# Opening of a decoder layer: modulation rows asked for one block sooner, ahead of the weight rows

## The chip, the core and the metric

The kernel runs on one core of a Trainium2 chip. The core has a matmul engine (TensorE, PE in the profile), a vector engine (VectorE, DVE), a scalar engine (ScalarE, ACT), a general engine (GpSimd, POOL) and a synchronization engine (SyncE, SP), which here only issues DMA transfers. The metric is the device time of one execution in microseconds, as the median over runs.

## The reference

One decoder layer over 512 positions with 1024 channels, all float32. What matters here is its beginning: a condition vector gives six modulation vectors, the first two of which shift and scale the normed input, and the result is multiplied by the columns of a large input projection.

```python
cond = jax.nn.silu(c)
mod = cond @ ada_w[l] + ada_b[l]
sh1, sc1, g1, sh2, sc2, g2 = jnp.split(mod[:, None, :], N_MOD, axis=-1)
u = rms_norm(x, mix_pre_g[l]) * (1.0 + sc1) + sh1
proj = u @ w_in[l]
...  # an mLSTM group and a convolution group, an output projection, then a ConvFFN
```

## The kernel before

Everything is computed with the channels on the 128 partitions. A product in float32 is made of three matmuls: each operand is split into a high part (fp32r, ACT) and a low part (the rest, POOL or DVE), and high by high, low by high and high by low are added up.

The stage that the change touches is called the opening. After the input is loaded, normed and turned, the opening goes over KT = 8 blocks of 128 input channels. For block k it needs

- the **modulation rows** of the block: `first_load(k)` loads two pieces of 512 KB (scale and shift, the two halves of one tile of 2048 columns) with two DMAs on SP's queue, line L245. The profile calls them `ada<-in_adaT`. The tiles lie in four buffers, two of the pool `raws` and two of the pool `early_raws`, so the load for block k takes the buffer of block k-4 and waits until the sums over it are done;
- the **weight rows** of the block: `w_rows(k)` loads 384 KB, the rows of the first G0 = 6 column tiles of the gated convolution's projection, with one DMA on SP's queue, line L343. The profile calls them `wglu<-in_w_glu`. There are two buffers (ADAS = 2), so the load for block k waits until the weight rows of block k-2 are split.

What is done with them: `w_part` splits the weight rows into high parts (ACT, L191, 512 columns and 256 columns) and low parts (POOL, L192). `part_sum` multiplies each modulation row by the condition and sums (DVE, L330, twice a block), `part_gains` makes a scale and a shift of the sums (L335, L336). ACT makes the high part of u from the turned input (L405), and again the full value (L406), and the low part is their difference (POOL, L407; in the last block DVE). Then `glu_pass` issues 18 matmuls for the block (L350): three passes over six banks that collect the sum over all blocks. On ACT, DVE and POOL the opening's instructions run in the order of the program (`in_order`), on ACT the two splits of a block ahead of its u. SP and PE run in the order of the program throughout. So SP, when the buffer of a load is not free, holds back all that stands behind it.

After the eight blocks the remaining projections follow (`proj`, line L210), then attention, convolution, output projection and the ConvFFN. The first load after the opening is that of the weights of column tile 3 (`glu_weights`, L199), which takes a buffer of `raws`.

Of the kernel before, what the change touches and what calls it, by code (L numbers as in the profile page):

```python
# [20 lines left out]
KT = D // P  # L21
# [34 lines left out]
def decoder_layer(ctx, tc, w_glu0, x, c, adaT, vecs, w_glu, w_qko, w_v0, w_vo, w_out, w_up, w_down, out):  # L56
# [93 lines left out]
    def vcols(name, i, n):  # L150
        a = VEC[name][0] + i
        return vec[:, a : a + n]
# [88 lines left out]
    def first_load(k):  # L241

        r = (raws if k % 4 < 2 else early_raws).tile([P, 2048], F32, tag="raw", name=f"ada{k}")
        for i in range(2):
            nc.sync.dma_start(r[:, i * D : (i + 1) * D], adaT[k][:, i * D : (i + 1) * D])  # L245
        first.append(r)
# [4 lines left out]
    def turn_x(j, tt):  # L251
        PE.transpose(xT_ps[j][:, tt * P : (tt + 1) * P], xn[tt][j // NT][:, j % NT * P : (j % NT + 1) * P], ident)
# [43 lines left out]
    def x_out(j, eng):  # L296
        if eng is S:
            S.activation(xr[j], xT_ps[j], AF.Copy)
        else:
            V.tensor_copy(xr[j], xT_ps[j])  # L300
# [23 lines left out]
    def part_sum(k, i):  # L324

        if i == 0:
            parts[k] = small.tile([P, 2], F32, tag="adap", name=f"adap{k}"), small.tile([P, 2], F32, tag="gsk", name=f"gsk{k}")
        part = parts[k][0]
        junk = small.tile([P, D], BF16, tag="junk", bufs=1, name=f"junk{k}_{i}")
        V.scalar_tensor_tensor(out=junk, in0=first[k][:, i * D : (i + 1) * D], scalar=1.0, in1=cps, op0=ALU.mult, op1=ALU.mult,  # L330
                               accum_out=part[:, i : i + 1])

    def part_gains(k):
        part, gsk = parts[k]
        V.tensor_scalar(out=gsk[:, :1], in0=part[:, :1], scalar1=bp1[:, k : k + 1], scalar2=g32[:, k : k + 1], op0=ALU.add, op1=ALU.mult)  # L335
        V.tensor_scalar(out=gsk[:, 1:], in0=part[:, 1:], scalar1=vcol("ada_b", 2 * k + 1), scalar2=None, op0=ALU.add)  # L336
# [4 lines left out]
    def w_rows(k):  # L341
        rows0[k] = adas.tile([P, D], F32, tag="ada", name=f"wglu0_{k}")
        nc.sync.dma_start(rows0[k][:, : G0 * P], w_glu0[k])  # L343

    def w_part(k, a, n):
        wk.append(w_split(rows0[k][:, a : a + n], f"wglu0_{k}_{a}"))

    def glu_pass(ps, i, p):
        a, b = ((0, 0), (1, 0), (0, 1))[p]
        PE.matmul(ps, blk(wk, i)[a], u[k][b], start=k == 0 and p == 0, stop=k == KT - 1 and p == 1)  # L350

    for k in range(KT):
        wk = []

        if k == 0:
            w_rows(0)
            first_load(1)
        if k + 1 < KT:
            w_rows(k + 1)
        if k + 2 < KT:  # L360
            first_load(k + 2)
        if k == 2:
            nc.sync.dma_start(vec[:, FIRST:], vecs[:, FIRST:])
        hi, lo = u[k]
        if k == 0:
            w_part(k, 0, T)
            part_sum(k, 0)
            part_sum(k, 1)
            part_gains(k)
            sc, sh = parts[k][1][:, :1], parts[k][1][:, 1:]  # L370
            S.activation(hi, xT_ps[0], AF.Identity, scale=sc, bias=sh)
            x_out(1, V)
            x_out(2, S)
            x_out(3, S)
            V.tensor_scalar(out=xr[0], in0=xT_ps[0], scalar1=sc, scalar2=sh, op0=ALU.mult, op1=ALU.add)
            G.tensor_tensor(out=lo, in0=xr[k], in1=hi.bitcast(F32), op=ALU.subtract)
            w_part(k, T, (G0 - 4) * P)
            x_out(4, V)
            x_out(5, S)
            for i, p in ((0, 0), (1, 0), (0, 1), (1, 1), (2, 0), (2, 1), (3, 0), (3, 1)):  # L380
                glu_pass(banks0[i], i, p)
            for j in range(6, KT):
                for tt in range(NT):
                    turn_x(j, tt)
            wk, first_wk = [], wk
            w_part(1, 0, T)
            wk, next_wk = first_wk, wk
            x_out(6, S)
            x_out(7, S)
            for i in range(4):  # L390
                glu_pass(banks0[i], i, 2)
            for p in range(3):
                for i in range(4, G0):
                    glu_pass(banks0[i], i, p)
        else:
            if k == 1:
                wk = next_wk
            else:
                w_part(k, 0, T)
            w_part(k, T, (G0 - 4) * P)  # L400
            part_sum(k, 0)
            part_sum(k, 1)
            part_gains(k)
            sc, sh = parts[k][1][:, :1], parts[k][1][:, 1:]
            S.activation(hi, xr[k], AF.Identity, scale=sc, bias=sh)  # L405
            S.activation(xr[k], xr[k], AF.Identity, scale=sc, bias=sh)  # L406
            (V if k == KT - 1 else G).tensor_tensor(out=lo, in0=xr[k], in1=hi.bitcast(F32), op=ALU.subtract)  # L407
            if k < KT - 1:
                for p in range(3):
                    for i, ps in enumerate(banks0):  # L410
                        glu_pass(ps, i, p)
            else:
                for i, ps in enumerate(banks0):
                    glu_pass(ps, i, 0)
                for i, ps in enumerate(banks0):
                    glu_pass(ps, i, 2)
                    glu_pass(ps, i, 1)
        if k == 6:
            V.tensor_scalar(out=cvw, in0=vcols("cv_dw_w", 0, CK * KT), scalar1=0.5, scalar2=None, op0=ALU.mult)
            V.tensor_scalar(out=ghalf, in0=vcols("ml_norm_g", 0, KT), scalar1=0.5, scalar2=None, op0=ALU.mult)  # L420
# [958 lines left out]
```

## Time and profile before

| | |
|---|---|
| median of 3 runs | 768.74 us (768.34 to 769.21) |
| profiled execution | 769.16 us |
| its span from first to last instruction | 767.4 us |
| PE busy | 756.0 us, 99% of the span |
| DVE, ACT, POOL busy | 576.6, 410.7, 516.5 us |
| mean granted clock of PE | 0.999 |
| loads of the opening on SP's queue | 16 modulation loads of 512 KB, 8 weight loads of 384 KB |
| first matmul of block 0, of the opening | 15.29 us |
| end of the opening's matmuls (first matmul of L210) | 51.02 us |

Times in the profile are microseconds from the first instruction; busy is the time in which an engine had an instruction running. A row of the timeline or of the chain gives start, length, engine, line and what is written from what. A row of the waits names the engine and line that waited, what it waited for, the total, the number of times and the longest. A row that describes transfers ends with the time from the issue to the landing of the data. The chain of work that ended last is followed back from the last instruction, at each step to what released it.

### The profile page before, as it was taken

How to read it: one execution, taken by the hardware profiler on the slowest of the kernel's cores; microseconds unless marked ns; L12 is line 12 of the kernel's file. 1: busy time of each engine (PE TensorE's matmuls, PEld its weight loads, DVE VectorE, ACT ScalarE, POOL GpSimd, SP SyncE). 2: the span in 40 equal slices, each digit the busy share in tenths (PEclk: the TensorE clock that was granted, in tenths of full speed). 3: DMA queues.
4: the chain of work that ended last, by engine and by line, in shares of the span. 5: the costliest groups of instructions: out<-in, count | busy, mean ns of one | idle time of the engine just before them, and what ended most of it. 6: DMA issues, size and time to landing. Idle time of an engine off the chain costs nothing.

```text
span 767.4 us, 10129 instructions
## 1 busy us (share of the span) xinstructions
PE 756.0 (99%) x3480; PEld 625.1 (81%) x3480; DVE 576.6 (75%) x837; ACT 410.7 (54%) x778; POOL 516.5 (67%) x428
## 2 busy tenths in 40 slices
PE   7999999999999999999999999999999999999996
PEld 5778898878788788888889988888888888888885
DVE  6669999979979696476989978675684775654547
ACT  6675428585665655573345444443534444566633
POOL 4779849796494872645631179786887884599943
PEclk9999999999999999999999999999999999999999
DMA  8973313411131241655965755666767565796273
GB/s 317 349 281 113 112 56 117 158 56 56 55 111 56 98 168 64 235 199 168 365 222 183 271 210 191 240 219 247 262 231 275 187 239 185 271 397 241 93 249 135
DMA packets 40136, 147.32 MB, mean 192 GB/s; under 512 B 3826, under 2 KB 5266, under 8 KB 30484
## 3 DMA queue, kind: packets, MB, share of 16 engines
q1 hardware_dynamic: 27524, 96.59, 34.9%
q10 hardware_dynamic: 12560, 50.08, 18.3%
q8 instruction: 27, 0.44, 0.2%
q14 instruction: 25, 0.20, 0.1%
HBM read 126.59 MB, written 20.07 MB: 191 GB/s over the span
## 4 chain that ended last, share of the span: by engine, by line
PE 93%; DMA 4%; POOL 1%; ACT 1%; issue 0%; DVEq 0%; SPq 0%; DVE 0%; POOLq 0%; ACTq 0%
PE up L210 31%; PE dn L210 13%; PE qko L210 13%; PE vo L210 9%; PE glu L210 7%; PE mixa L210 6%; PE mixb L210 6%; DMA wglu<-in_w_glu 3%; PE o L562 2%; PE s L551 2%; PE v L210 2%; PE glu L350 1%; DMA xn<-in_x 1%; PE xT L992 0%; PE hT L593 0%
## 5 line engine op out<-in xcount | busy, mean ns | idle before, releaser
L774 DVE SCALAR_TENSOR_TENSOR cv<-gt,cvw,cv 128x485 f32<-128x485 f32 (+24 forms) x200 | 137.2, 731 | 2.1 <-ACT cv L762 0.8
L770 POOL TENSOR_TENSOR cs<-cs,cs 128x510 f32<-128x510 f32 (+3 forms) x32 | 42.1, 1316 | 0.2
L192 POOL TENSOR_TENSOR wup_0l<-wup,wup_0h 128x512 fp32r<-128x512 f32 x18 | 25.0, 1389 | 19.4 <-ACT wup_0h L191 19.3
L210 PE MATMUL up<-u2h,wup_0h 128*128 128x512 f32 (+1 forms) x96 | 35.8, 373 | 0.0
L210 PE MATMUL up<-u2h,wup_0l 128*128 128x512 f32 (+1 forms) x96 | 35.7, 371 | 0.0
L210 PE MATMUL up<-u2h,wup_512h 128*128 128x512 f32 (+1 forms) x96 | 35.6, 371 | 0.0
L210 PE MATMUL up<-u2l,wup_512h 128*128 128x512 f32 (+1 forms) x96 | 35.6, 371 | 0.0
L210 PE MATMUL up<-u2h,wup_512l 128*128 128x512 f32 (+1 forms) x96 | 35.6, 371 | 0.0
L210 PE MATMUL up<-u2l,wup_0h 128*128 128x512 f32 (+1 forms) x96 | 35.6, 371 | 0.0
L210 PE MATMUL up<-u2h,wup_1024h 128*128 128x512 f32 (+1 forms) x92 | 35.0, 381 | 0.0
L210 PE MATMUL up<-u2l,wup_1024h 128*128 128x512 f32 (+1 forms) x92 | 34.9, 380 | 0.0
L210 PE MATMUL up<-u2h,wup_1536l 128*128 128x512 f32 (+1 forms) x92 | 34.9, 380 | 0.0
L210 PE MATMUL up<-u2h,wup_1536h 128*128 128x512 f32 (+1 forms) x92 | 34.9, 380 | 0.0
L210 PE MATMUL up<-u2l,wup_1536h 128*128 128x512 f32 (+1 forms) x92 | 34.9, 380 | 0.0
L210 PE MATMUL up<-u2h,wup_1024l 128*128 128x512 f32 (+1 forms) x92 | 34.9, 380 | 0.0
L176 DVE SCALAR_TENSOR_TENSOR junk<-ada,cb 128x1024 bf16<-128x1024 f32 x20 | 29.9, 1493 | 2.6 <-DMA ada<-in_adaT 2.5
L768 ACT ACTIVATE cs<-gt,cvw 128x511 f32<-128x511 f32 (+4 forms) x40 | 27.1, 713 | 6.1 <-POOL cs L770 3.5
L192 POOL TENSOR_TENSOR wup_1536l<-wup,wup_1536h 128x512 fp32r<-128x512 f32 x18 | 24.6, 1365 | 6.0 <-ACT wup_1536h L191 5.4
L191 ACT ACTIVATE wup_512h<-wup 128x512 fp32r<-128x512 f32 x22 | 13.8, 629 | 25.7 <-PE up L210 20.9
L192 POOL TENSOR_TENSOR wup_1024l<-wup,wup_1024h 128x512 fp32r<-128x512 f32 x18 | 23.6, 1314 | 5.0 <-ACT wup_1024h L191 5.0
L330 DVE SCALAR_TENSOR_TENSOR junk<-ada,cps 128x1024 bf16<-128x1024 f32 x16 | 19.5, 1220 | 9.8 <-DMA ada<-in_adaT 9.2
L1113 DVE TENSOR_TENSOR b<-b 128x512 f32<-128x512 f32 x11 | 19.4, 1762 | 8.6 <-POOL b L1112 8.6
(1097 smaller groups left out, 2726.8 us busy)
## 6 DMA issues: line engine op xcount, KB each, us to landing
wup<-in_w_up SPq DMA_DIRECT2D x22, 1024.0 KB, 5.0
b<-in_w_down ACTq DMA_DIRECT2D x11, 1024.0 KB, 5.1
spill_t<-b ACTq DMA_DIRECT2D x11, 1024.0 KB, 3.9
ada<-in_adaT ACTq DMA_DIRECT2D x20, 512.0 KB, 4.8
wqko<-in_w_qko SPq DMA_DIRECT2D x9, 1024.0 KB, 4.8
ada<-in_adaT SPq DMA_DIRECT2D x16, 512.0 KB, 7.5
wo<-in_w_out SPq DMA_DIRECT2D x8, 1024.0 KB, 5.5
wvo<-in_w_vo SPq DMA_DIRECT2D x6, 1024.0 KB, 4.8
```

What stands on the lines that cost most here:

```text
L176: t = V.scalar_tensor_tensor(out=junk, in0=r, scalar=1.0, in1=cb, op0=ALU.mult, op1=ALU.mult, accum_out=mod[:, i : i + 1])
L191: S.activation(hi[:, :n], src, AF.Copy)
L192: (eng or G).tensor_tensor(out=lo[:, :n], in0=src, in1=hi[:, :n].bitcast(F32), op=ALU.subtract)
L210: PE.matmul(ps, l, r, start=start and i == 0, stop=stop and i == 2, skip_group_check=again)
L330: V.scalar_tensor_tensor(out=junk, in0=first[k][:, i * D : (i + 1) * D], scalar=1.0, in1=cps, op0=ALU.mult, op1=ALU.mult, accum_out=part[: ...
L350: PE.matmul(ps, blk(wk, i)[a], u[k][b], start=k == 0 and p == 0, stop=k == KT - 1 and p == 1)
L551: PE.matmul(sp[:, :n], ks[d][:, cc * P : (cc + 1) * P], qs[d][:, cc * P :], start=d == 0, stop=d == 1)
L562: PE.matmul(o[:, : DH + 2], E[h][cc][:, a : a + P], vs[h][cc], start=cc == 0, stop=cc == tt)
L768: S.activation(t[:, d:], cvx[j][:, : T - d], AF.Copy, scale=w(CK - 1 - d))
L770: G.tensor_tensor(out=side[:, d:], in0=side[:, d:], in1=t[:, d:], op=ALU.add)
L774: tap = V.scalar_tensor_tensor(out=cp[:, d:], in0=cvx[j][:, : T - d], scalar=w(CK - 1 - d), in1=cp[:, d:], op0=ALU.mult, op1=ALU.add)
L1113: V.tensor_tensor(out=b22, in0=b22, in1=b11, op=ALU.subtract)
```

## The change

In the loop over the blocks, the loads are issued in another order. Before, block k asked for the weight rows of block k+1 and then for the modulation rows of block k+2. After, block 0 also asks for the modulation rows of block 3, and each later block k asks first for the modulation rows of block k+3 and then for the weight rows of block k+1. What is loaded, into which buffers, and what is computed stays as it is.

```diff
         if k == 0:
             w_rows(0)
             first_load(1)
-        if k + 1 < KT:
+        if k == 0:
+            w_rows(1)
+            first_load(2)
+        if k + 3 < KT:
+            first_load(k + 3)
+        if 0 < k < KT - 1:
             w_rows(k + 1)
-        if k + 2 < KT:
-            first_load(k + 2)
         if k == 2:
             nc.sync.dma_start(vec[:, FIRST:], vecs[:, FIRST:])
```

## The prediction

> **What bounds the kernel now.** I read the page's busy times first, then the chain that ended last, then the waits of the matmul engine after the opening, then the opening alone: chain, transfers, throughput.
>
> ```profile
> span 767.4 us, 10129 instructions
> PE 756.0 (99%) x3480; PEld 625.1 (81%) x3480; DVE 576.6 (75%) x837; ACT 410.7 (54%) x778; POOL 516.5 (67%) x428
> PE 93%; DMA 4%; POOL 1%; ACT 1%; issue 0%; DVEq 0%; SPq 0%; DVE 0%; POOLq 0%; ACTq 0%
> ```
>
> PE is the bound: 93% of the chain is PE, and the rest has to be sought where PE does not yet run without a break. The waits of PE show two in the opening and, asked from 52 us to the end, none:
>
> ```profile
> PE glu L350 <- ACT uh L371: 1.3, 1, 1.3
> PE glu L350 <- ACT uh L405: 0.9, 1, 0.9
> ```
>
> So whatever PE loses or wins before its last L350 matmul passes on to the end, one for one. The chain in time from 17 to 51 us:
>
> ```profile
> 17.41 0.74 POOL wglu_512l L192
> 18.16 0.02 issue
> 18.18 3.60 DMA wglu<-in_w_glu
> 21.77 0.02 issue
> 21.80 0.64 ACT wglu_0h L191
> ...
> 24.52 7.04 DMA wglu<-in_w_glu
> ...
> 41.03 0.63 ACT wglu_0h L191
> ...
> 42.72 8.45 PE glu L350 x36
> ```
>
> The reader sees a loop: weight rows of block k land, ACT and POOL split them, the buffer comes free, SP issues the weight rows of block k+2, and these wait in the queue for their turn. The chain runs through the weight rows (wglu), never through the modulation rows (ada). The last wait ends at 42.72, with block 6; block 7 starts at 46.94 and the stage ends at 51.02.
>
> **The change, part by part.** It adds and removes no instruction and no byte: on SP's queue two modulation loads per block (512 KB each) change places with one weight load. I write m_k for the pair of modulation loads of block k, w_k for its weight load. Before: m2, w2, m3, w3, m4, vec, w4, m5, w5, m6, w6, m7, w7. After: m2, m3, m4, w2, m5, w3, vec, m6, w4, m7, w5, w6, w7.
>
> *What it wins.* SP stands at w2 until POOL has finished with the first buffer (the 17.41 row), and nothing is queued behind it. The second half of m2 and w2:
>
> ```profile
> 11.39 0.33 SPq L245 DMA_DIRECT2D ada<-in_adaT  x1
> ada<-in_adaT SPq DMA_DIRECT2D x1, 512.0 KB, 8.5
> 18.18 0.33 SPq L343 DMA_DIRECT2D wglu<-in_w_glu  x1
> wglu<-in_w_glu SPq DMA_DIRECT2D x1, 384.0 KB, 3.6
> ```
>
> m2 lands at 11.39 + 8.5 = 19.9, and w2, with an empty queue, 3.6 after its issue. Throughput (columns: window, its length, granted clock, DMA share, GB/s):
>
> ```profile
> 11.00:18.40 7.40, 1.00 1.03 411
> 18.50:20.00 1.50, 1.00 0.71 141
> 37.00:41.00 4.00, 1.00 0.86 263
> ```
>
> Between 18.5 and 20 the engines moved 141 GB/s where 411 is usual: 1.5 x (1 - 141/411) = 1.0 us of transfer time lost. With m3 and m4 issued ahead of the wait this hole is filled. Also the vector engine's waits for modulation rows shrink:
>
> ```profile
> ACT wglu_0h L191 <- DMA wglu<-in_w_glu: 12.6, 8, 3.4
> DVE junk L330 <- DMA ada<-in_adaT: 9.2, 7, 2.1
> ```
>
> I cost that at nothing. ACT scales block k into u behind its split of w_k, so the later of the two rows decides, and that is the wglu row. Its cover is w_k arriving late; were w_k early, the modulation sums would be last.
>
> *Can the moved loads go out in time?* m4 needs the buffer of m0, read by block 0's sums, the last of which ends at 14.05:
>
> ```profile
> 13.97 0.08 DVE L330 DVE_READ_ACCUMULATOR junk<-ada,cps 128x1 f32 x1
> 4.86 0.33 SPq L245 DMA_DIRECT2D ada<-in_adaT  x1
> ada<-in_adaT SPq DMA_DIRECT2D x1, 512.0 KB, 6.5
> 7.59 0.33 SPq L245 DMA_DIRECT2D ada<-in_adaT  x1
> ada<-in_adaT SPq DMA_DIRECT2D x1, 512.0 KB, 7.5
> ```
>
> m2's second half went out at 11.39, when the first half of m0, eight transfers ahead of it in issue order, had landed (4.86 + 6.5 = 11.4). By that rule m4's second half waits for the first half of m1: 7.59 + 7.5 = 15.1. SP is back at the wait for w2 long before 18.18, which therefore stays its issue time. Nothing waits behind it that did not before.
>
> *What it costs.* At 18.18 the queue now holds the rest of m2 and all of m3 and m4. Transfers of this queue landed in the order of issue, so w2 follows four more halves. These and w2 are 4 x 0.524 + 0.393 = 2.49 MB, at 411 GB/s 6.1 us after m2's 19.9: w2 lands at 26.0 instead of 21.8. That is the lower end. For the upper end:
>
> ```profile
> 27.32 0.63 ACT L191 ACTIVATE wglu_0h<-wglu 128x512 fp32r<-128x512 f32 x1 [3.03 <-DMA wglu<-in_w_glu]
> 29.02 1.21 PE L350 MATMUL glu<-uh,wglu_0h 128*128 128x512 f32 x4
> q8 instruction: 1, 0.02, 6.2%
> ```
>
> From w2 (21.8, in the chain) to w3 there were 5.5 us for 1.44 MB, which at 411 GB/s take 3.5. The 2.0 too many lie in the very time in which w2 will now be on its way. The last row, of the transfers from 24.3 to 25.3, names one contributor, an instruction fetch that took a turn on one of the sixteen engines, and a load has landed only when all sixteen are done. Some of the 2.0 came of the queue's fresh start at 19 and will go. So w2 lands between 26.0 and 28.0; I take 26.8, a little under the middle of the two, for that share.
>
> The Trainium skill, "DMA: Bandwidth & Descriptors", section "Bandwidth", says that loads from HBM are bound at about 358 GB/s per core. By that the 2.49 MB take 7.0 us, w2 lands at 26.9 without any stall, and the sum below would be 0.9 longer at its lower end. The 411 GB/s of this trace disagree, and I do not use it.
>
> *The path.* From the start of ACT's split to the block's first matmul it is 29.02 - 27.32 = 1.70 us (42.72 - 41.03 = 1.69 in block 6). PE per block (columns as above, with PE's busy time and count):
>
> ```profile
> 20.67:24.75 4.08, 4.08 (x20) 1.00 1.01 356
> 37.54:42.72 5.18, 4.24 (x19) 1.00 0.91 301
> 42.72:46.94 4.22, 4.22 (x19) 1.00 1.01 424
> 46.94:51.02 4.08, 4.08 (x19) 1.00 0.76 296
> ```
>
> A block takes 4.08, and 4.22 after a wait. Block 1 ends at 24.75 as before, since w0, m0, w1 and m1 are ahead of all that moves. Block 2 then starts at 26.8 + 1.7 = 28.5 after 3.8 us of idleness, and six blocks follow: 28.5 + 4.22 + 5 x 4.08 = 53.1. Against 51.02 that is **+2.1 us**; the bounds of w2 make it +1.3 and +3.3. Break-even is w2 landing at 24.7.
>
> *What is late next.* w3 comes 1.44 MB behind w2, 3.5 us, and PE needs it 4.2 after: 0.7 to spare. w4 has vec's 0.3 MB as well, 1.74 MB or 4.2 us against 4.1: 0.6 left. w5 takes 3.5 of 4.1: 1.2 left. w6 and w7 have no modulation rows between them any more; w6 waits for the buffer of w4, which is free 2.7 us after that landed (21.80 to 24.52 in the chain, on block 2), plus 3.6 for an empty queue = 6.3, against 8.2 that PE needs for two blocks. So the wait of block 6 before (5.18 - 4.24 = 0.94) disappears, and the price is paid once, in block 2.
>
> **The rivals.**
> *Later stall.* The 263 GB/s of 37 to 41 lose 4 x (1 - 263/411) = 1.4 us. If such a stretch now strikes while w4 or w5 is on its way, 0.6 of slack covers some and 0.8 is added: +2.9, 771.6. For it: block 6's late start before came of it. Against: from 11 to 18.4 there was no such stretch.
>
> *Slow restart of PE.* Eight transposes took 1.91 us at 8.75 and 1.04 at 11.41, at the same granted clock:
>
> ```profile
> 8.75 1.91 PE L267 MATMUL xT<-ident 128*128 128x128 f32 x8
> 11.41 1.04 PE L267 MATMUL xT<-ident 128*128 128x128 f32 x8
> ```
>
> So PE starts at about half its pace after being idle. If 3.8 us of idleness bring that back for one block, it costs 4.08 x (1.91/1.04 - 1) = 3.4 more: +5.5, 774.2. Against: block 6, after its wait, took only 0.14 longer than one without. The Trainium skill, "TensorE: Matmul & The Clock Gate", "Part 1: The HAM clock gate", says that the clock is halved after a whole free-running window of about 3.4 us without work; by that, 3.8 us of idleness would rarely hold a whole window, and by its half pace for one window the price would be 1.7. The two transpose rows agree with the half pace; no idle time that long stands here later.
>
> *No effect.* If the transfers are served so that w2 does not wait for what was queued ahead, or if the order of service hides it, block 2 starts as before: 768.7. Against: the landings above follow the order of issue.
>
> *Faster.* The hole at 18.5 is filled and w2 still lands by 23.0, so that block 2 starts at 24.75 without a wait; then all later waits go: 24.75 + 6 x 4.08 = 49.2, that is -1.8, 766.9. It decides from w2 landing before 24.7. For it: 1.0 us of transfer time regained. Against: 2.1 MB more in front of w2 are 5.1 us.
>
> **How the numbers follow.** The profiled execution took 769.16 us for a span of 767.4, 1.8 of it around the span; the median of the runs is 768.74, 0.4 lower. The sum makes 771.3 of the former, and I predict the median: 768.74 + 2.1 = **770.8**. 0.2% is 1.5 us, about what a measurement can tell here. Chances: late w2 0.62 (own range 770.0 to 772.0), later stall 0.12, slow restart 0.08, no effect 0.10, faster 0.08. Of the 0.62, the part with w2 landing before 26.2 is within 0.2%, which I put at 0.15. Slower by over 0.2%: 0.47 + 0.12 + 0.08 = 0.67; within: 0.15 + 0.10 + 0.03 (a gain that comes in part) = 0.28; faster: 0.05. The range 768.5 to 773.0 leaves out the slow restart and the gain, some 0.17.
>
> **What the changed profile would show.** Right: w2 issued at about 18.2 and landing 8 to 9 us later; one wait of PE of 3 to 4 us before block 2, then six blocks of 4.1 with no wait; the vector engine's waits for ada nearly gone; a full transfer rate from 18.5 to 20. Wrong, if w2 lands before 24.7, if PE waits before several blocks, if block 2 takes over 4.5, or if PE waits anywhere after the last L350 matmul.

## The result: slower, by more than twice the forecast

| | before | changed |
|---|---|---|
| median | 768.54 us (6 runs, 767.48 to 769.21) | 773.85 us (6 runs, 771.99 to 774.98) |
| ratio, 95% interval | | 1.0065 (1.0049 to 1.0081) |
| profiled execution, its span | 769.16 us, 767.4 us | 774.98 us, 773.3 us |
| mean granted clock of PE | 0.999 | 0.994 |
| first matmul of L210 (end of the opening) | 51.02 us | 55.80 us |

The change makes the kernel 5.3 us slower, where +2.1 was forecast and the range ended at 773.0. The profiled execution of the changed kernel is the slowest of its six, which spread over 3 us; a reason that fits is seen below. Each ratio below is to the kernel before on the same chip, whose medians in the three groups of runs were 768.63, 768.63 and 768.33 us. In the text m2 stands for the modulation rows of block 2, w2 for its weight rows, and so on, as in the prediction.

The chain of the changed kernel in time, to be read against the one of before:

```profile
17.11 0.74 POOL wglu_512l L192
17.85 0.02 issue
17.87 9.03 DMA wglu<-in_w_glu
26.90 0.02 issue
26.92 0.63 ACT wglu_0h L191
27.55 0.31 ACT wglu_512h L191
27.86 0.71 ACT uh L408
28.57 0.04 issue
28.61 27.35 PE glu L350 x108
```

w2 is issued as early as before, and takes 9.03 us instead of 3.60. After that the weight rows are never last again: from 28.61 all 108 matmuls of the six blocks left run in one piece. The waits of ACT for weight rows and of DVE for modulation rows over the opening:

```profile
ACT wglu_0h L191 <- DMA wglu<-in_w_glu: 13.1, 8, 6.1
DVE junk L330 <- DMA ada<-in_adaT: 2.7, 4, 1.4
```

DVE's waits went from 9.2 to 2.7 us, which is what the edit is about; ACT's went from 12.6 to 13.1, of which 6.1 are now one piece. PE by stretches (window, length, PE's busy time and count, granted clock, DMA share, GB/s):

```profile
18.50:20.00 1.50, 1.50 (x8) 1.00 1.01 404
24.43:28.61 4.18, 0.15 (x1) 0.84 1.02 400
28.61:35.40 6.79, 6.79 (x18) 0.59 1.01 379
35.40:39.48 4.08, 4.08 (x19) 1.00 0.54 190
47.64:51.72 4.08, 4.08 (x19) 1.00 0.92 369
```

The hole at 18.5 to 20 is filled (404 GB/s against 141). Ahead of block 2 PE is idle for 4.03 us (4.18 less 0.15), and then block 2 takes 6.79 us, at a mean granted clock of 0.59. The other blocks take 4.08.

PE's matmuls stand in the same order in both kernels, so their starts can be subtracted one by one. The changed kernel is 0.3 us ahead at the end of block 1 (24.43 against 24.75), 3.9 behind at the start of block 2, 6.4 at the start of block 3 (35.40 against 29.02), 4.8 at the end of the opening, since the waits of before in blocks 3 to 6 are gone, 5.4 at the matmuls of the forget gates (`fcum`, 133.19 against 127.82), and 5.8 in the whole execution (774.98 against 769.16).

### The profile page after: what moved, and what is told of

Same layout as the page of the kernel before. It is cut to its first block, busy times and chain, and to the rows that moved or that the text cites. A ratio compares the mean times of both kernels' runs of the same rounds, so it can differ in the third digit from the quotient of the medians.

```text
span 773.3 us, 10129 instructions
## 1 busy us (share of the span) xinstructions
PE 758.1 (98%) x3480; PEld 626.6 (81%) x3480; DVE 575.8 (74%) x837; ACT 411.4 (53%) x778; POOL 518.0 (67%) x428
## 4 chain that ended last, share of the span: by engine, by line
PE 90%; DMA 4%; DVE 2%; ACT 1%; issue 1%; POOL 1%; DVEq 0%; SPq 0%; POOLq 0%; ACTq 0%
PE up L210 31%; PE qko L210 11%; PE dn L210 10%; PE vo L210 8%; PE glu L210 7%; PE mixa L210 6%; PE mixb L210 6%; PE glu L350 4%; PE o L565 2%; PE s L554 2%; DMA wglu<-in_w_glu 2%; DMA p<-spill_t 1%; PE v L210 1%; DMA xn<-in_x 1%; PE hT L596 0%
## 5 line engine op out<-in xcount | busy, mean ns | idle before, releaser
L777 DVE SCALAR_TENSOR_TENSOR cv<-gt,cvw,cv 128x485 f32<-128x485 f32 (+23 forms) x200 | 137.2, 732 | 2.2 <-ACT cv L765 0.8
L210 PE MATMUL up<-u2h,wup_0h 128*128 128x512 f32 (+1 forms) x96 | 35.8, 373 | 0.0
L210 PE MATMUL up<-u2h,wup_0l 128*128 128x512 f32 (+1 forms) x96 | 35.7, 371 | 0.0
L210 PE MATMUL up<-u2h,wup_512h 128*128 128x512 f32 (+1 forms) x96 | 35.6, 371 | 0.0
L210 PE MATMUL up<-u2l,wup_512h 128*128 128x512 f32 (+1 forms) x96 | 35.6, 371 | 0.0
L210 PE MATMUL up<-u2h,wup_512l 128*128 128x512 f32 (+1 forms) x96 | 35.6, 371 | 0.0
L210 PE MATMUL up<-u2l,wup_0h 128*128 128x512 f32 (+1 forms) x96 | 35.6, 371 | 0.0
L210 PE MATMUL up<-u2h,wup_1024h 128*128 128x512 f32 (+1 forms) x92 | 35.0, 381 | 0.0
L210 PE MATMUL up<-u2l,wup_1024h 128*128 128x512 f32 (+1 forms) x92 | 34.9, 380 | 0.0
L210 PE MATMUL up<-u2h,wup_1536l 128*128 128x512 f32 (+1 forms) x92 | 34.9, 380 | 0.0
L210 PE MATMUL up<-u2h,wup_1536h 128*128 128x512 f32 (+1 forms) x92 | 34.9, 380 | 0.0
L210 PE MATMUL up<-u2l,wup_1536h 128*128 128x512 f32 (+1 forms) x92 | 34.9, 380 | 0.0
L210 PE MATMUL up<-u2h,wup_1024l 128*128 128x512 f32 (+1 forms) x92 | 34.9, 380 | 0.0
L192 POOL TENSOR_TENSOR wup_512l<-wup,wup_512h 128x512 fp32r<-128x512 f32 x18 | 24.2, 1346 | 0.5 <-ACT wup_512h L191 0.5
```

Source lines behind the costliest of these rows:

```text
L192: (eng or G).tensor_tensor(out=lo[:, :n], in0=src, in1=hi[:, :n].bitcast(F32), op=ALU.subtract)
L210: PE.matmul(ps, l, r, start=start and i == 0, stop=stop and i == 2, skip_group_check=again)
L777: tap = V.scalar_tensor_tensor(out=cp[:, d:], in0=cvx[j][:, : T - d], scalar=w(CK - 1 - d), in1=cp[:, d:], op0=ALU.mult, op1=ALU.add)
```

## The experiments

Theory A, after the result: w2 is late because m3 and m4 are on their way ahead of it; PE's idleness is the first part of the price, and the clock that is halved because of this idleness is the second.

**Keeping PE busy, e1_keepwarm.** Sixteen matmuls with zero weights, which add zero to a bank, in front of block 2 (shortened; the tile of zeros is made ahead of the loop).

```diff
+            if k == 2:
+                for _ in range(16):
+                    PE.matmul(banks0[0], nil.to_broadcast([P, P]), u[0][0], start=False, stop=False, ...)
```

> The changed order, with 16 matmuls of zero weights on PE in front of block 2 (they add zero to a bank), so that PE is not idle while it waits for w2. Theory A (the loss is the wait for w2, and on top of it the half clock which PE's idleness brings): w2 still lands at about 26.9 and block 2 starts at about 28.6, but the granted clock stays at 1.0, block 2 takes 4.1 to 4.3 us instead of 6.8, and the time is 2.6 us below the changed kernel's, about 771.2. Rival B (PE is slow in block 2 for another reason, such as slow operands or contention, not because it idled): block 2 still takes about 6.8 us and the time stays at 773.9.

Measured: 771.86 us, ratio 1.0042 (1.0025 to 1.0059). PE's timeline in this kernel:

```profile
25.21 3.87 PE L415 MATMUL glu<-uh,nil 128*128 128x512 f32 x16
28.91 1.08 PE L352 MATMUL glu<-uh,wglu_0h 128*128 128x512 f32 x4
```

Block 2 as one stretch (window, length, PE's busy time and count, granted clock, DMA share, GB/s):

```profile
28.91:33.00 4.09, 4.09 (x19) 1.00 1.01 402
```

Block 2 starts 0.3 us later than in the changed kernel (its w2 split begins at 26.94) and takes 4.09 us at full clock. The idleness is what halves the clock, and in the profile that part of the price is 6.79 - 4.09 = 2.7 us. The medians differ by 2.0 (773.85 against 771.86). Rival B falls.

**Fewer halves ahead of w2.** Three orders on the same chip, with two, three and one half of modulation rows between m2 and w2 (the edits are shortened).

```diff
 # e2_two_halves: m3 ahead of w2, every later m(k+3) behind w(k+1)
-        if k + 3 < KT:
+        if 0 < k and k + 3 < KT:   # moved below w_rows(k + 1); first_load(3) in block 0
 # e3_three_halves: m3, then half of m(k+3), w(k+1), the other half
+            first_load(k + 3, (0,)); w_rows(k + 1); first_load(k + 3, (1,))
 # e4_one_half: half of m3, then w(k+1), the half of m(k+2) that is left, half of m(k+3)
+            w_rows(k + 1); first_load(k + 2, (1,)); first_load(k + 3, (0,))
```

> m3 alone (two halves) goes ahead of w2; m4 and all later modulation rows stay behind the weight rows. Theory A: w2 lands 2.6 us earlier than in the changed kernel, at about 24.3, block 2 starts at about 26.0 after 1.6 us of idleness, the granted clock stays at 1.0, and with no wait later the stage ends at 26.0 + 24.6 = 50.6: 768.1, equal to before within 0.5. Rival D (what costs is that the modulation rows are asked for sooner at all, by contention or because the planner orders the other engines otherwise): about +1 or more, 769.5 or above.

> One half of m(k+3) goes ahead of w(k+1) and the other half behind it, m3 whole ahead: three halves ahead of w2. Theory A: w2 lands 1.3 us earlier than in the changed kernel, at about 25.6, block 2 starts at about 27.3 after 2.9 us of idleness. If the clock halves only after a longer idleness, it stays at 1.0 and the stage ends at about 51.9: 769.4 (+0.9). If 2.9 us are enough, block 2 takes up to 2.6 us more: 772. Rival D: no difference to the changed kernel beyond 0.5, 773.5.

> Only the first half of m(k+3) is asked for sooner, and one half stands ahead of w2. Theory A: it fills the hole of the queue at 18.5 to 20 almost exactly, w2 lands at about 23.0, block 2 starts at about 24.7 without a wait, the wait of block 6 goes or shrinks: stage end 49.5 to 50.5, time 767 to 768 (-0.5 to -1.5). Rival D: +0.5 or more.

The start of ACT's split of w2, from ACT's timeline in three kernels; the last value is ACT's wait ahead of it. First e4_one_half:

```profile
22.29 0.63 ACT L191 ACTIVATE wglu_0h<-wglu 128x512 fp32r<-128x512 f32 x1 [1.10 <-DMA wglu<-in_w_glu]
```

The same row in e2_two_halves:

```profile
23.11 0.63 ACT L191 ACTIVATE wglu_0h<-wglu 128x512 fp32r<-128x512 f32 x1 [2.38 <-DMA wglu<-in_w_glu]
```

And in e3_three_halves:

```profile
24.35 0.63 ACT L191 ACTIVATE wglu_0h<-wglu 128x512 fp32r<-128x512 f32 x1 [3.66 <-DMA wglu<-in_w_glu]
```

| halves ahead of w2 | 0 (before) | 1 | 2 | 3 | 4 (changed) |
|---|---|---|---|---|---|
| split of w2 starts | 21.80 | 22.29 | 23.11 | 24.35 | 26.92 |
| PE's waits in front of blocks 2 to 7 (first matmul) | 0.9 | none | 0.7 | 1.8 | 4.0 |
| end of the opening | 51.02 | 49.36 | 50.38 | 51.42 | 55.80 |
| median | 768.6 | 771.17 | 769.27 | 771.13 | 773.85 |
| ratio to before | | 1.0029 (1.0017 to 1.0041) | 1.0010 (1.0000 to 1.0020) | 1.0041 (1.0028 to 1.0054) | 1.0065 (1.0049 to 1.0081) |

The weight load is late by the transfer time of what stands ahead of it: the first half mostly fits into the hole (0.5 us), and the second and third cost 0.8 and 1.2, where 524 KB at 411 GB/s take 1.28. The fourth costs 2.6, and half of that is something else. In the trace of the changed kernel 120 of the 128 packets of w2 are through by 25.19 us, and the last eight, a sixteenth, only at 26.44; from 23.74 to 24.83 a fetch of 16 KB of instructions took one of the sixteen transfer engines. The trace does not name a packet's engine, so that it was the same one is inferred. But with one and two halves w2 was through before the fetch began, and in e12_short_filler below, which has the changed kernel's order, the fetch came behind w2, at 26.06, and the split of w2 began at 26.17 instead of 26.92. So some 0.75 to 1.2 us of w2's delay come of the fetch, into which the new order moved it, and the rest of the bytes ahead.

The whole of the changed kernel's wait in front of these blocks can thus be taken away by order alone, 4.0 us to none with one half. But none of the three times came as expected: two halves missed by 1.2 us (768.1 expected), three halves by 1.7 (769.4), and one half, which has the best opening, by over 3 (767 to 768); it ends 2.5 us above before. For two and three halves the cause is open: the profiles caught executions of 768.52 and 770.35 us, without a halved clock. Of the ten executions of e3_three_halves four took 772.56 to 773.62 and six at most 771.21; a halved clock in those four would fit, and no profile shows it.

In e4_one_half PE waits again far behind the opening, by the waits of PE:

```profile
PE fcum L664 <- DVE g_lf L625: 1.7, 1, 1.7
```

and by its stretches there:

```profile
126.83:130.24 3.41, 2.25 (x14) 1.00 0.36 86
130.24:133.65 3.41, 3.41 (x10) 0.50 0.54 226
```

The gain of the opening brings PE earlier to the cumulative sum of the forget gates, whose input `g_lf` DVE finishes no sooner (127.94 us, in the kernel before 127.11), and behind that wait the clock is halved for 3.41 us. The wait and the 1.7 us of the half clock are more than the 1.7 us won.

**The gates later.** The block of `fcum` is issued behind the third projection of head 0 instead of in front of it, with the one-half order and, as a control, with the order of before. Theory A2: what e4_one_half lost is the wait at `fcum` and the clock halved behind it.

```diff
+    head_proj(0, 2)
     fps = atbank("fcum")
...
-    head_proj(0, 2)
```

> The order with one half sooner (as in e4_one_half), and PE's matmuls of the forget gates' cumulative sum (fcum) issued behind the third projection of head 0 instead of in front of it. Theory A2 (the opening of e4_one_half gains 1.5 us by PE's offsets, and the 3.5 us lost at 128 are PE's wait for g_lf, made late by the planner's order of the vector engine, plus the clock halved by that wait): no wait at fcum, granted clock 1.0 throughout, time 767.1 (-1.5). Rival D2 (what is won in the opening is always lost again behind it, whatever waits are taken away): 768.6 or above.

> Control: the kernel before with only fcum issued behind the third projection. PE did not wait at fcum before, so Theory A2 expects no change, 768.6 within 0.5. If this alone gains 1 us or more, the gain of e5_half_gates_later is not the opening's.

Measured: 768.17 us, ratio 1.0004 (0.9995 to 1.0012), and the control 768.01, 0.9996 (0.9988 to 1.0005). The wait at `fcum` is gone and so are 3.0 us of e4_one_half's 771.17, as theory A2 has it. But the 1.6 us won in the opening, which this profile shows too (its opening ends at 49.43), are not in the median: both are equal to before. This was missed, and why is open. The profile of e5_half_gates_later is 1.3 us shorter than that of before (767.86 against 769.16), so in these two executions the gain passes on; but the runs of before lie between 767.15 and 769.69, and its profiled one is near their upper end. One profile of the control shows that such executions differ in ways that the order does not set:

```profile
13.44:16.85 3.41, 1.51 (x6) 1.00 1.02 409
16.85:20.26 3.41, 3.41 (x14) 0.50 0.86 281
```

Here the clock was halved at the start of block 0, where PE waits for 0.4 to 2.2 us in the profiles (1.9 here), and this execution took 769.67 us.

**The other queue.** The weight rows of blocks 2 to 7 go to ACT's queue, in the changed order; the second kernel has the gates later as well.

```diff
-        nc.sync.dma_start(rows0[k][:, : G0 * P], w_glu0[k])
+        (nc.scalar if k > 1 else nc.sync).dma_start(rows0[k][:, : G0 * P], w_glu0[k])
```

> The changed order, with the weight rows of blocks 2 to 7 issued on ACT's DMA queue instead of SP's, so that w2 does not stand behind m3 and m4 in one queue, though the same bytes are under way. Theory A (w2 is late because transfers of one queue are served in order): two queues share the transfer engines, w2 is issued at about 18.5 and lands at about 22 to 23.5 instead of 26.9, block 2 starts at 24.5 to 25.2 with no clock halving, and the time is 767 to 769, 5 us below the changed kernel. Rival E (w2 is late because the engines are saturated with four more halves, whatever the queue): w2 lands at 26 or later and the time stays above 771.

> e7_other_queue with fcum issued behind the third projection of head 0. Theory A2: equal to e7_other_queue where that shows no wait at fcum, and up to 2 us faster where it does; 766.5 to 768. Rival E: above 771.

Measured: 775.34 (1.0097, 1.0080 to 1.0114) and 775.74 (1.0096, 1.0083 to 1.0110). ACT's rows in e7_other_queue, the issue and the split of w2, and the split of w4:

```profile
18.19 0.33 ACTq L343 DMA_DIRECT2D wglu<-in_w_glu  x1
25.97 0.63 ACT L191 ACTIVATE wglu_0h<-wglu 128x512 fp32r<-128x512 f32 x1 [5.31 <-DMA wglu<-in_w_glu]
38.26 0.63 ACT L191 ACTIVATE wglu_0h<-wglu 128x512 fp32r<-128x512 f32 x1 [4.86 <-DMA wglu<-in_w_glu]
```

That part of theory A which spoke of one queue is wrong in the main: w2 in a queue of its own had its first packet under way at 21.69, 3.5 us after its issue, and was split 7.8 us after it, only 0.95 sooner than in the changed kernel. What stands ahead is the backlog of the shared transfer engines, rival E. Here, too, the instruction fetch (23.67 to 24.76) has a share: fifteen of the sixteen parts of w2 had landed by 23.99, the last at 25.50. Without it, an estimate from these two figures, the other queue would have had w2 ready at about 24.5. Later w4 came 3.6 us later than in the changed kernel, and PE waited twice; in e8_other_queue_gates_later it waited three times.

**Moving the wait, e9_w2_first.** w2 goes ahead of m3 and m4, and w3 behind m3, m4 and m5 (shortened).

```diff
+        if k == 1:
+            w_rows(2); first_load(3); first_load(4)
-        if k + 3 < KT:
+        if 1 < k and k + 3 < KT:
             first_load(k + 3)
-        if 0 < k < KT - 1:
+        if 1 < k < KT - 1:
             w_rows(k + 1)
```

> The changed order, but w2 ahead of m3 and m4; m5 then stands ahead of w3 with them. Theory A (a weight load lands when the bytes issued before it are through): w2 lands at about 21.8 and block 2 starts without a wait, but six halves now stand ahead of w3, which lands at 30.4 to 32; PE waits 3.3 to 4.9 us in front of block 3 instead, and the clock halves again: stage end 54.3 to 56.8, time 772 to 774.5. Rival F (the wait belongs to the time at which w2 was issued, or to the instruction fetch at 24, not to the bytes ahead): with w2 early the loss is gone, 768 to 769.

Measured: 775.91 us, 1.0105 (1.0082 to 1.0128), 1.4 us above the expected upper end (774.5). The splits of w2 and w3 in ACT's timeline:

```profile
21.34 0.63 ACT L191 ACTIVATE wglu_0h<-wglu 128x512 fp32r<-128x512 f32 x1 [0.61 <-DMA wglu<-in_w_glu]
31.87 0.63 ACT L191 ACTIVATE wglu_0h<-wglu 128x512 fp32r<-128x512 f32 x1 [8.04 <-DMA wglu<-in_w_glu]
```

PE's wait for them, in its own timeline:

```profile
33.57 2.07 PE L350 MATMUL glu<-uh,wglu_0h 128*128 128x512 f32 x4 [4.95 <-ACT uh L412]
```

and the halved stretch that follows:

```profile
32.50:39.33 6.83, 5.76 (x14) 0.50 0.80 317
```

The wait moved one block on with the bytes and grew with them, and the halved clock went with it. Rival F falls: the wait belongs neither to the time at which w2 is issued nor to the instruction fetch alone (24.57 to 25.56 here, well ahead of the first packet of w3 at 28.42). What the fetch adds to the changed kernel's wait is said above.

**The rest.** The changed kernel with the gates later, the changed kernel again, and the changed kernel with 8 zero matmuls, on one chip.

> The changed kernel with fcum issued behind the third projection of head 0. Theory A: the offsets of PE against the kernel before show 4.9 us at the end of the opening and 0.45 more at fcum; only the 0.45 goes, 773.4. Rival D (the order of the other engines behind the opening carries a good part of the loss): 771.5 or less.

> The changed kernel itself, on the chip of the other runs of this call, so that they can be set against it: 773.9, that is +5.3 to the kernel before.

> As e1_keepwarm with 8 zero matmuls instead of 16: PE is idle for about 2.4 us before block 2 instead of 4. If the clock halves only after an idle window of 3.4 us, it stays at 1.0, and the time equals e1_keepwarm, 771.9. If about 2 us of idleness can be enough, depending on how they fall into the window, some executions show one halved window: 772 to 773.5, between e1_keepwarm and the changed kernel.

| | median | ratio |
|---|---|---|
| e11_changed_again | 774.63 | 1.0082 (1.0067 to 1.0097) |
| e10_changed_gates_later | 773.08 | 1.0064 (1.0047 to 1.0081) |
| e12_short_filler | 771.79 | 1.0045 (1.0030 to 1.0060) |

The loss is there again. With the gates later it is 1.5 us smaller, between the two expectations; the intervals overlap, so a share of about 1 us for the wait at `fcum` is likely and not proven. e12_short_filler equals e1_keepwarm, and lies 2.8 us below e11_changed_again. Its profile cannot tell whether 2.4 us of idleness are harmless, since in that execution the clock was halved in block 0 already, which made block 1 end later and filled the gap. In the profile of e11_changed_again the clock is halved for one window, not two:

```profile
26.20:29.61 3.41, 1.03 (x4) 1.00 1.03 403
29.61:33.02 3.41, 3.41 (x10) 0.50 1.02 402
```

and against it the profile of the changed kernel:

```profile
23.89:27.30 3.41, 0.69 (x4) 1.00 1.01 398
27.30:34.13 6.83, 5.52 (x13) 0.50 1.01 384
```

6.83 is two times 3.41. Where the windows fall against the wait differs from execution to execution, and one or two of them are halved, at 1.7 us each for a busy PE; this fits the spread of 3 us in the changed kernel's times.

Not every window with a gap is followed by a halved one. Counted back in steps of 3.41 us from the halved stretch of e8_other_queue_gates_later, this window was not:

```profile
26.05:29.46 3.41, 1.74 (x8) 1.00 1.03 404
29.46:32.87 3.41, 3.15 (x14) 1.00 1.02 407
```

PE was busy for less of it than of the 2.25 us in e4_one_half, so busy time does not draw the line. But those 2.25 us hold eight matmuls of at most 16 columns. If one counts the columns that PE went through, at 4.08 / 18 = 0.227 us for 512, the window of e4_one_half holds 1.3 us of work and this one 1.6. Counted so, with the transposes of the beginning at the pace of their own rows (1.04 us for eight), the windows of all fourteen traces part: those with up to 1.39 us were followed by a halved one, those with 1.44 or more were not. The line at about 1.4 of 3.41 is an estimate, and no run was made to test it.

## Why the prediction was wrong

*Right: the late weight load.* w2 was forecast to land at 26.8 and landed at 26.9, block 2 to start at 28.5 and started at 28.6. The moved loads went out in time, w2's issue did not move, the hole of 18.5 to 20 was filled, and the waits of all later blocks went as forecast. The small slacks of w3 to w5 held, and not only because block 2 was slow: in e1_keepwarm, where it took 4.09, no later block waits either. That w2 landed within 0.1 us of the forecast has some luck in it: the 0.8 us taken for stalls was a choice between bounds, and in e12_short_filler, without the fetch on its way, w2 was split at 26.17.

*Wrong: "block 2 takes 4.22, a block after a wait".* This term measured 6.79 us, 2.6 more. The runs showed in its place a clock halved because PE had idled for 4.0 us: e1_keepwarm, without the idleness, has block 2 at 4.09. The mechanism stood among the rivals as the slow restart, with a price of 3.4 and a chance of 0.08, and it was dismissed on block 6's restart after a wait of 0.94 us, although the sum itself had PE idle for 3.8. The price was of the right order; it was the chance that failed, and with it the sum, which should have held the term. The rows of the transposes were also misread: "at the same granted clock" has no ground, since the clock record of that trace begins at 11.07 us, after the first of the two rows (8.75). The argument that 3.8 us would rarely hold a whole window of 3.4 is refuted by the runs: halving needs no whole idle window. Ahead of the halved stretches PE had been busy for 0.69, 1.03, 1.51 and 2.25 us of 3.41 in the four profiles shown. The Trainium skill, "TensorE: Matmul & The Clock Gate", "Part 1: The HAM clock gate", gives the length of the window, 3.4 us, which these rows show, 3.41; its condition of a whole idle window they do not.

*Wrong: "whatever PE loses or wins before its last L350 matmul passes on, one for one".* After the opening 1.0 us more was lost, of 5.8 in the profiles: 0.6 by `fcum`, the rest at the end.

```profile
PE fcum L661 <- DVE g_lf L622: 0.4, 1, 0.4
```

The page of before shows no wait there, so it told nothing of how little slack DVE had. From about 49 us on DVE, ACT and POOL run their instructions in another order in the two traces, although the edit does not touch that part. e4_one_half is the same failure with the other sign: its 1.7 us of gain were eaten there. Where PE does not wait at `fcum`, the step holds: against the profile of before, e1_keepwarm is 2.4 us behind at the end of the opening and 2.3 at the end, e10_changed_gates_later 3.7 and 3.7.

*The sum as measured.* Forecast: 2.1. Measured at the end of the opening: 4.8, which is 2.1 + 2.6 and 0.1. With 1.0 behind it the profiled execution is 5.8 longer, the median 5.3.

## What to carry to other kernels

A load that waits for its buffer does not only hold back what stands behind it: once it goes, it pays for every byte that was let past it, so what is moved ahead should be no more than the hole it is to fill (here one half of 512 KB, not four; and even that gave no gain in the median). Price a wait of the matmul engine together with the clock that the wait takes away: here windows of 3.41 us with 1.2 to 2.7 us of idleness were followed by halved ones, at 1.7 us each for a busy PE, though another with 1.7 us was not. And a profile without waits at a place says nothing of the slack there; an engine that arrives 1.5 us earlier may find the others not ready.

## What the runs showed of the hardware

The clock was halved for one or two stretches of 3.41 us, after windows of that length in which PE had been busy for at most 2.25 us; a wait of 1.7 us in front of small matmuls was enough in e4_one_half. A window with 1.74 us of large matmuls in e8_other_queue_gates_later was not followed by a halved one; by the columns gone through, the line is estimated at about 1.4 us. The halving also struck at block 0, in single executions of e6_before_gates_later and e12_short_filler. A second DMA queue did not let a load of 384 KB past a backlog of some 2 MB: 7.8 us from issue to use, against 9.0 in the same queue and 3.6 without a backlog. And a fetch of 16 KB of instructions, 1.09 us on one transfer engine, went with the last sixteenth of a load coming 1.2 us (changed kernel) and 1.5 us (e7_other_queue) after the other fifteen.
